# Hybrid encoder step: which gates are projected plainly, a buffer for the LayerNorm's squares, and where the down operands lie

## The chip, the cores and the metric

The kernel runs on one core of one Trainium2 chip. The metric is the device time of one launch in microseconds, median of several executions.

## The reference, cut to what matters

One layer of a hybrid encoder runs on 1024 prompt frames and 64 new frames of another stream, 1088 tokens in all, with model width 1024 in float32. A normalised input `h` is multiplied with one wide matrix. The columns of the product feed four branches of width 512, a SiLU gate for each, and four merge gates of width 1024:

```
h = rms_norm(x, norm_pre);  P = h @ w_in
A: RG-LRU        u_a = lru(conv4(lru_x)) * silu(lru_g)
B: SSD           u_b = rms_norm(ssd(silu(conv4(xbc))) * silu(ssd_z), ssd_norm)
C: conv module   u_c = silu(layer_norm(conv31(glu(cf_in)))) * silu(cf_g)
D: attention     u_d = stick_breaking(q, k, v) * silu(sb_g)
m = sum over b of sigmoid(P_merge_b) * (u_b @ w_down[b])
y = x + rms_norm(m @ w_out, norm_post)
```

The states of the convolutions, of the LRU and of the SSD, and all keys and values, are outputs too.

## The kernel before

Channels lie on the partitions and tokens on the free axis. `hh` and `hl`, each [128, 8, 1088], hold `h` as a rounded high part and the rest (the kernel calls such a pair hi and lo); a product of two such pairs is three matmuls (`mm3`, or the triple at line 721). A column group of 128 is called a chunk; weights come from DRAM by `weights` or `Pair.prepare` and are split into hi and lo by ScalarE and VectorE (`split`, lines 228 and 229).

The stages, in order of time:

1. Head, attention, convolutions: plain projection in three token pieces (`SPL`: 384, 384, 320 tokens). It ends with four chunks by `spill`, which applies SiLU and stores the gate in DRAM. Before the change these are the SSD gates `sz` (C_SZ).
2. Pairs: 20 `Pair` objects, each two chunks by Strassen's scheme of seven products (`ORDER` = 1, 2, 6, 5, 7, 3, 4). The tokens are split in two halves of 544 (`tlo`, `thi`), the contraction in `k0` and `k1`; a product reads one quadrant pair: products 1, 2, 3, 4 read `hh` and `hl` at (k0, tlo), (k1, tlo), (k1, thi), (k0, thi), the others separate tiles T6, T5, T7. A product is 24 matmuls of 272 columns. Two pairs make the LayerNorm gates `cg` (C_CG), two the LRU gates `lg`, 16 the merge gates `mgs`; `done` applies SiLU where asked and stores `r`. Six banks of PSUM serve them.
3. Beside the pairs runs a generator, `chains()`. After each product `step` calls `next(side)`, so that its work is emitted between products: `wait(15)`, then `layer_norm` (four quarters of 272 tokens), `lru` (eight half chunks), `ssd` (nine chunks of 128 tokens: seg, join of the chunk before, scores, norm of the chunk before, turn, off, diag). A `yield` ends a step. There are 140 products, so 140 calls; what is left is called at once after the pairs (line 1078).
4. Down products: for each branch in the order 3, 0, 2, 1 the operand `u` is loaded from DRAM (`uh_d`, `ul_d`), eight output chunks `d` of it are multiplied in the pieces of `SPL`, and VectorE multiplies each with the sigmoid of a merge gate (`load_gate`, tiles `sga`) and adds up in `m`. `us[0]` is loaded into a pool on the right side of SBUF, where the SSD's pool was; `us[1]` and `us[2]` into the places of `hh` and `hl`.
5. Output product, norm and residual in 9 token tiles.

TensorE's instructions keep the order in which the program emits them (`manual_schedule`); the other engines' and the DMA queue's (all DMAs are issued from SP) are ordered by a planner with priorities (`high_priority`). Every queue is in order. A tile of a pool of one buffer is written again only when its last reader is done.

In `layer_norm` the lines that matter are:

```
sq = ln.tile([128, 4, QT], FT, name="lnq")
S.activation(sq, X, AF.Square)                 # line 775
a = fold(sq)                                   # lines 755, 756
yield from wait(2)
p = pg()[:, :QT]
PE.matmul(p, ones, a, start=True, stop=True)   # line 779
...
gh = ln.tile([128, 4, QT], FR, name="lnh", tag="lnq")
split(gh, gw, X)
dma(uh_d[2][:, :, t], gh.bitcast(FT))          # line 793
```

`lnh` and `lnq` are one buffer by their tag. Line 772 is the first matmul of a quarter (the sum for the mean), 773 subtracts the mean, 781 to 789 finish the norm.

Of the kernel before, what the change touches and what calls it, by code (L numbers as in the profile page):

```python
# [8 lines left out]
FT = mybir.dt.float32  # L9
FR = mybir.dt.float32r  # L10
# [35 lines left out]
def encoder_step(ctx, tc, x, prm, win, wdt, wdn, wout, lwa, lwx, ckT, cv_, ssd0, npre, npost, dtb, alog, dskip,  # L46
# [534 lines left out]
    def spill(chunk, dst):  # L581
        def evac(t0, n, p):
            g = tmp.tile([128, NM], FT, name="t3", bufs=3)
            S.activation(g[:, :n], p[:, :n], AF.Silu)  # L584
            dma(dst[:, t0:t0 + n], g[:, :n])
        yield from proj(chunk, evac)

    feed.add(*(spill(C_SZ + c, sz_d[:, c]) for c in range(4)))
    feed.step(1)
    tlo, thi = slice(0, HT), slice(HT, T)  # L590
    k0, k1 = slice(0, 4), slice(4, 8)
# [146 lines left out]
            dma(dst[:, c + e, f * HT:f * HT + HT], r)  # L738
        return Pair(base + c, base + c + 1, done, func or AF.Copy)

    pairs = [stored(C_CG, c, cg_d, AF.Silu) for c in (0, 2)] + [stored(C_LG, c, lg_d, AF.Silu) for c in (0, 2)]
    pairs += [stored(C_MG, 2 * i, mg_d) for i in range(16)]

    def wait(n):
# [4 lines left out]
    def layer_norm():  # L749
        lnp = ExitStack()  # L750
        ln = lnp.enter_context(tc.tile_pool(name="ln", bufs=1, side="right", reuse_waits="tile"))

        def fold(t_):
            a = ln.tile([128, 2, QT], FT, name="lns", bufs=2)
            V.tensor_tensor(a, t_[:, 0:2], t_[:, 2:4], op=OP.add)
            V.tensor_tensor(a[:, 0], a[:, 0], a[:, 1], op=OP.add)
            return a[:, 0]

        def load(q):
            X = ln.tile([128, 4, QT], FT, name="lnx", bufs=2)  # L760
            dma(X, cv_d[:, :, q * QT:q * QT + QT])
            return X, fold(X)

        nxt = load(0)
        yield from wait(3)
        for q in range(4):
            t = slice(q * QT, q * QT + QT)
            X, a = nxt
            gl = ln.tile([128, 4, QT], FT, name="lng")
            dma(gl, cg_d[:, :, t])  # L770
            p = pg()[:, :QT]
            PE.matmul(p, ones, a, start=True, stop=True)
            V.scalar_tensor_tensor(X, p[:, None, :].to_broadcast([128, 4, QT]), -1.0 / 512, X, op0=OP.mult, op1=OP.add)
            sq = ln.tile([128, 4, QT], FT, name="lnq")
            S.activation(sq, X, AF.Square)
            a = fold(sq)
            yield from wait(2)
            p = pg()[:, :QT]
            PE.matmul(p, ones, a, start=True, stop=True)
            rs = ln.tile([128, QT], FT, name="lnr")  # L780
            S.activation(rs, p, AF.Sqrt, bias=eps_t, scale=1.0 / 512)
            V.reciprocal(rs, rs)
            V.tensor_tensor(X, X, rs[:, None, :].to_broadcast([128, 4, QT]), op=OP.mult)
            if q < 3:
                nxt = load(q + 1)
            for c in range(4):
                V.tensor_scalar(X[:, c], X[:, c], P("lg", c), P("lb", c), op0=OP.mult, op1=OP.add)
            S.activation(X, X, AF.Silu)
            V.tensor_tensor(X, X, gl, op=OP.mult)
            gh = ln.tile([128, 4, QT], FR, name="lnh", tag="lnq")  # L790
            gw = ln.tile([128, 4, QT], FR, name="lnl", tag="lng")
            split(gh, gw, X)
            dma(uh_d[2][:, :, t], gh.bitcast(FT))
            dma(ul_d[2][:, :, t], gw.bitcast(FT))
            yield from wait(3)
        lnp.close()


    def lru():
# [31 lines left out]
            pass  # L831
        todo = [(c, j) for c in range(4) for j in range(2)]
        nxt = load(0, 0)
        yield from wait(2)
        for m, (c, j) in enumerate(todo):
            t = slice(j * HT, j * HT + HT)
            xc, xh, xl = nxt
# [201 lines left out]
        p3.close()  # L1039

    def chains():
        yield from wait(15)
        yield from layer_norm()
        yield from lru()
        yield from ssd()
# [22 lines left out]
    for n, pair in enumerate(pairs):  # L1068
# [6 lines left out]
                pairs[n + 1].prepare()  # L1075
            next(side, None)
        pair.run(next_weights, step)
    while next(side, left) is not left:
        pass


    order = (3, 0, 2, 1)
    put = ExitStack()
    ut = put.enter_context(tc.tile_pool(name="ut", bufs=1, side="right", reuse_waits="tile"))

    def load_u(bi, pool, **kw):
        u = pool.tile([128, 2, 4, T], FR, name=f"u{bi}", **kw)
        for e, src in enumerate((uh_d, ul_d)):
            for t0, n in SPL:
                dma(u[:, e, :, t0:t0 + n].bitcast(FT), src[order[bi]][:, :, t0:t0 + n])  # L1090
        return u

    us = [load_u(0, ut, tag="u")]
    nwd = weights(wdn[order[0], 0])
    a1.close()
    ps2.close()
# [2 lines left out]
    def pj():  # L1099
        return ps.tile([128, 512], FT, name="pj3", bufs=6)  # L1100

    tp_ = ctx.enter_context(tc.tile_pool(name="tp", bufs=3, reuse_waits="tile"))
    mp = ctx.enter_context(tc.tile_pool(name="mp", bufs=1, reuse_waits="tile"))
    mt = [mp.tile([128, T], FT, name=f"m{d}") for d in range(8)]
    sgp = ctx.enter_context(tc.tile_pool(name="sgp", bufs=1, reuse_waits="tile"))
# [7 lines left out]
    def down(wh, wl, e, u, t0, n):  # L1113
        p = pj()
        for k in range(4):
            mm3(p[:, :n], wh[:, 4 * e + k, :], wl[:, 4 * e + k, :], u[:, 0, k, t0:t0 + n], u[:, 1, k, t0:t0 + n], k == 0, k == 3)
        return p

    gates = [load_gate(order[0], d) for d in range(8)]
    us += [load_u(1, hp, tag="hh"), load_u(2, hp, tag="hl")]  # L1120
    ml = []
    for bi, b in enumerate(order):
        u = us[bi]
        if bi == 1:
            us.append(load_u(3, ut, tag="u"))
        if bi == 3:
            mh = hp.tile([128, 8, T], FR, name="mh", tag="hh")
            wo0 = hp.tile([128, 8, 1024], FR, name="wo0", tag="hl")
            wo = [[wo0[:, d] for d in range(8)], []]
        for d in range(8):  # L1130
            if d % 2 == 0:
                wh, wl = nwd
            g = gates[d]
            for i, (t0, n) in enumerate(SPL):
                p = down(wh, wl, d % 2, u, t0, n)
                m, gi = mt[d][:, t0:t0 + n], g[:, t0:t0 + n]
                if bi == 0:
                    V.tensor_tensor(m, p[:, :n], gi, op=OP.mult)
                else:
                    V.tensor_tensor(gi, p[:, :n], gi, op=OP.mult)  # L1140
                    if bi < 3:
                        V.tensor_tensor(m, m, gi, op=OP.add)
                    else:
                        V.tensor_tensor(gi, m, gi, op=OP.add)
                        S.activation(mh[:, d, t0:t0 + n], gi, AF.Copy)
                if i == 0 and d % 2 and (d < 7 or bi < 3):
                    nwd = weights(wdn[b, d // 2 + 1] if d < 7 else wdn[order[bi + 1], 0])
            if bi < 3:
                gates[d] = load_gate(order[bi + 1], d)
                continue  # L1150
            l_ = mp.tile([128, T], FR, name=f"ml{d}", tag=f"m{d}")
            V.tensor_sub(l_, g, mh[:, d].bitcast(FT))
            ml.append(l_)
            wo[1].append(sgp.tile([128, 1024], FR, name=f"wp{d}", tag=f"sga{d}"))
            raw = wp.tile([128, 1024], FT, name="w_raw", bufs=2)
            dma(raw, wout[d])
            for e in range(2):
                w = wo[e][d]
                split(w[:, 0:512], w[:, 512:1024], raw[:, e * 512:e * 512 + 512])
    put.close()  # L1160
    ut = ctx.enter_context(tc.tile_pool(name="op", bufs=1, side="right", reuse_waits="tile"))
    gp_bc = ut.tile([128, D], FT, name="gp_bc")
    dma(gp_bc, ap(npost, 0, [[0, 128], [1, D]]))
    for i in range(9):
        r = 128 if i < 8 else 64
        xr = ut.tile([128, D], FT, name="xr", bufs=2)
        dma(xr[:r], x[i * 128:i * 128 + r, :])
        st = tp_.tile([128, 4], FT, name="ost", bufs=2)
        sq = ut.tile([128, 512], FT, name="osq")
        yo = ut.tile([128, D], FT, name="yo", bufs=2)  # L1170
        for e in range(2):
            p = pj()
            for k in range(8):
                w = wo[e][k]
                mm3(p[:r], mh[:, k, i * 128:i * 128 + r], ml[k][:, i * 128:i * 128 + r], w[:, 0:512], w[:, 512:1024],
                    k == 0, k == 7)
            S.activation(sq[:r], p[:r], AF.Square, accum_out=st[:r, e:e + 1])
            es = slice(e * 512, e * 512 + 512)
            V.tensor_tensor(yo[:r, es], p[:r], gp_bc[:r, es], op=OP.mult)
        V.tensor_tensor(st[:r, 0:1], st[:r, 0:1], st[:r, 1:2], op=OP.add)  # L1180
        rstd(st, r, D)
        for e in range(2):
            es = slice(e * 512, e * 512 + 512)
            V.scalar_tensor_tensor(yo[:r, es], yo[:r, es], st[:r, 1:2], xr[:r, es], op0=OP.mult, op1=OP.add)
            dma(y_o[i * 128:i * 128 + r, es], yo[:r, es])
# [63 lines left out]
```

## Time and profile before

| | us |
|---|---|
| median of 3 runs | 1520.71 (1520.14 to 1522.0) |
| profiled execution | 1520.43 |
| its span, first to last instruction | 1518.6 |
| TensorE busy | 1417.0 (93%) |
| VectorE busy | 1060.6 (70%) |
| ScalarE busy | 676.1 (45%) |
| mean granted TensorE clock | 0.972 |

Busy time of TensorE is the union of overlapping matmul records; whether it runs at its pace is read from the count of matmuls in a window. The granted clock is a share of 2.4 GHz, and its two levels are 1.00 and 0.50.

### The profile page before, as it was taken

The page shows a single profiled execution, that of the slowest core. Times are in us where ns is not written, and L with a number is a line of the kernel's source. Part 1 is how long each engine was busy: PE and PEld are TensorE (multiplying, and loading weights), DVE is VectorE, ACT ScalarE, POOL GpSimd, SP SyncE. Part 2 cuts the span into 40 slices and gives each one's busy share as a digit, 9 for nine tenths or more (in the row PEclk, how much of TensorE's full clock was granted, in tenths as well). Part 3 has the DMA queues.
Part 4 walks back from the last instruction along what each step waited for, and adds up shares of the span by engine and source line. Part 5 has one row for each costly group of instructions (what it writes and reads, how often), then busy time and mean ns, then how long its engine had stood idle before and what let it go on. Part 6 is the DMA issues. An engine that isn't in the chain of part 4 may idle for free.

```text
span 1518.6 us, 24934 instructions
## 1 busy us (share of the span) xinstructions
PE 1417.0 (93%) x9665; PEld 1352.7 (89%) x9665; DVE 1060.6 (70%) x1604; ACT 676.1 (45%) x1227; POOL 262.4 (17%) x245
## 2 busy tenths in 40 slices
PE   6999999999999999899788999999999289999998
PEld 6899999999999897899788989999999189999885
DVE  6299799789779977645776867787776324669433
ACT  6324543544454454344556885344444412224211
POOL 0002221231231226322211313131220000000000
PEclk9999999999999999999898999999999589999999
DMA  5222222213213233133444445434343987443322
GB/s 205 74 85 64 69 70 80 82 36 105 84 53 94 65 100 93 51 105 121 161 162 156 149 158 154 141 120 142 118 131 111 329 276 244 148 133 124 111 84 70
DMA packets 121206, 184.41 MB, mean 121 GB/s; under 512 B 22272, under 2 KB 82560, under 8 KB 121088
## 3 DMA queue, kind: packets, MB, share of 16 engines
q1 hardware_dynamic: 121088, 182.82, 37.5%
q8 instruction: 76, 1.25, 0.4%
q14 instruction: 42, 0.34, 0.1%
HBM read 118.00 MB, written 60.59 MB: 118 GB/s over the span
## 4 chain that ended last, share of the span: by engine, by line
PE 43%; DVE 6%; DMA 4%; ACT 4%; issue 1%; SPq 0%; DVEq 0%; ACTq 0%
PE bank L721 19%; PE pj L110 7%; PE pj L111 7%; PE pj L109 7%; DVE w_lo L229 1%; DMA sga<-mgs 1%; ACT w_hi L228 1%; DMA u<-ul 1%; DMA uh<-uoh 1%; DMA ul<-uol 1%; DVE gx L860 1%; ACT L852 1%; PE pg L965 0%; DMA uh<-lnh 0%; PE pg L912 0%
## 5 line engine op out<-in xcount | busy, mean ns | idle before, releaser
L109 PE MATMUL pj<-hh,w_hi 128*128 128x384 f32 (+3 forms) x960 | 317.8, 331 | 6.7 <-ACT t L584 5.4
L110 PE MATMUL pj<-hl,w_hi 128*128 128x384 f32 (+3 forms) x960 | 315.3, 328 | 1.6 <-DVE hl L225 1.6
L111 PE MATMUL pj<-hh,w_lo 128*128 128x384 f32 (+3 forms) x960 | 315.1, 328 | 0.0
L721 PE MATMUL bank<-hh,w_hi 128*128 128x272 f32 x640 | 191.8, 300 | 3.2 <-ACT t L584 1.8
L109 PEld LDWEIGHTS pj<-hh,w_hi 128*128 128x128 f32 x960 | 182.2, 190 | 9.5 <-ACT t L584 5.5
L721 PE MATMUL bank<-hl,w_hi 128*128 128x272 f32 x640 | 186.8, 292 | 0.0
L721 PE MATMUL bank<-hh,w_lo 128*128 128x272 f32 x640 | 186.8, 292 | 0.0
L110 PEld LDWEIGHTS pj<-hl,w_hi 128*128 128x128 f32 x960 | 182.1, 190 | 3.6 <-DVE hl L225 2.5
L111 PEld LDWEIGHTS pj<-hh,w_lo 128*128 128x128 f32 x960 | 181.9, 189 | 0.2
L243 DVE SCALAR_TENSOR_TENSOR cvo<-cbuf,p_t,cvo 128x1118 f32<-128x1118 f32 x120 | 165.5, 1379 | 1.8
L721 PE MATMUL bank<-Th,w_hi 128*128 128x272 f32 x480 | 141.3, 294 | 1.5 <-ACT r L725 1.5
L109 PE MATMUL pj<-u,w_hi 128*128 128x384 f32 (+1 forms) x384 | 126.3, 329 | 13.8 <-DMA u<-uh 13.8
L721 PE MATMUL bank<-Th,w_lo 128*128 128x272 f32 x480 | 138.4, 288 | 0.0
L721 PE MATMUL bank<-Tl,w_hi 128*128 128x272 f32 x480 | 138.2, 288 | 0.0
L110 PE MATMUL pj<-u,w_hi 128*128 128x384 f32 (+1 forms) x384 | 126.4, 329 | 6.4 <-DMA u<-ul 6.4
L721 PEld LDWEIGHTS bank<-hh,w_hi 128*128 128x128 f32 x640 | 123.3, 193 | 5.5 <-ACT t L584 2.0
L111 PE MATMUL pj<-u,w_lo 128*128 128x384 f32 (+1 forms) x384 | 126.3, 329 | 0.0
L721 PEld LDWEIGHTS bank<-hl,w_hi 128*128 128x128 f32 x640 | 123.1, 192 | 0.8
L721 PEld LDWEIGHTS bank<-hh,w_lo 128*128 128x128 f32 x640 | 122.8, 192 | 0.0
L460 POOL TENSOR_SCALAR_AFFINE_SELECT fb<-fb 128x128 f32<-128x128 f32 (+1 forms) x72 | 38.5, 535 | 453.7 <-ACT fb L455 329.3
L101 ACT ACTIVATE w_hi<-w_raw 128x1024 fp32r<-128x1024 f32 x56 | 59.4, 1061 | 113.6 <-PE pj L110 106.5
L463 DVE TENSOR_TENSOR_SCAN fb<-fb,ones 128x128 f32<-128x128 f32 (+8 forms) x68 | 90.1, 1325 | 27.9 <-POOL fb L460 27.8
(339 smaller groups left out, 2982.2 us busy)
## 6 DMA issues: line engine op xcount, KB each, us to landing
w_raw<-in_win_dram SPq DMA_DIRECT2D x80, 512.0 KB, 3.8
mgs<-r SPq DMA_DIRECT2D x64, 272.0 KB, 2.5
sga<-mgs SPq DMA_DIRECT2D x32, 544.0 KB, 3.8
w_raw<-in_wdn_dram SPq DMA_DIRECT2D x16, 512.0 KB, 4.4
u<-uh SPq DMA_DIRECT2D x8, 768.0 KB, 6.6
u<-ul SPq DMA_DIRECT2D x8, 768.0 KB, 10.7
xt<-in_x_dram SPq DMA_DIRECT2D x8, 512.0 KB, 9.2
xbc<-xc SPq DMA_DIRECT2D x8, 512.0 KB, 2.7
```

The lines of the kernel that those rows point to most:

```text
L101: S.activation(hi, r3, AF.Copy)
L109: PE.matmul(out, ah, bh, start=first, stop=False)
L110: PE.matmul(out, ah, bl, start=False, stop=False)
L111: PE.matmul(out, al, bh, start=False, stop=last)
L228: S.activation(hi, src, AF.Copy)
L229: V.tensor_sub(lo, src, hi.bitcast(FT))
L243: V.scalar_tensor_tensor(out[:, :n], b[:, i:i + n], w[:, i:i + 1], out[:, :n], op0=OP.mult, op1=OP.add)
L460: G.affine_select(t_[s, 1024 - w:1024], t_[s, 1024 - w:1024], pattern=[[-1, w]], compare_op=OP.is_gt, fill=fill, base=0, channel_multiplier=1)
L463: V.tensor_tensor_scan(F[:, rev], F[:, rev], ones[:, 0:1].to_broadcast([128, n]), 1.0, OP.mult, OP.mult)
L721: PE.matmul(p, a_[:, k], b_[:, k, s], start=new and k == 0 and z == 0, stop=k == 3 and z == 2, skip_group_check=True)
L852: S.activation(ga, gr, AF.Exp, scale=lm8[:, c:c + 1])
L860: V.tensor_tensor_scan(gx[:, :n], ga[:, :n], gx[:, :n], hp_ if j else 0.0, OP.mult, OP.add)
```

## The change

- The LayerNorm gates are projected plainly in stage 1, and the SSD gates as two pairs, after the two of the LRU gates.
- `chains()` starts without `wait(15)`; in `layer_norm` and `lru` one `wait(2)` each becomes `wait(3)`.
- `lnh` has a buffer of its own.
- The call that finishes the side work after the pairs is moved: one call per piece in the first branch of the down products, the rest at the start of the second.
- `us[0]` and `us[1]` are laid into the four quarters of `hh` and `hl` over (k0, k1) and one token half each; these two operands are multiplied in four pieces of 272 tokens. `us[2]` goes into a tile on the right, loaded at the start of the second branch; `us[3]` into `hl`, loaded at the start of the third. The high part of the mix stays in `hh`, and the output stage's buffers are parts of a tile in the place of `hl`.

```
-    feed.add(*(spill(C_SZ + c, sz_d[:, c]) for c in range(4)))
+    feed.add(*(spill(C_CG + c, cg_d[:, c]) for c in range(4)))
...
-    pairs = [stored(C_CG, c, cg_d, AF.Silu) for c in (0, 2)] + [stored(C_LG, c, lg_d, AF.Silu) for c in (0, 2)]
+    pairs = [stored(C_LG, c, lg_d, AF.Silu) for c in (0, 2)] + [stored(C_SZ, c, sz_d, AF.Silu) for c in (0, 2)]
     pairs += [stored(C_MG, 2 * i, mg_d) for i in range(16)]
...  layer_norm
             a = fold(sq)
-            yield from wait(2)
+            yield from wait(3)
...
-            gh = ln.tile([128, 4, QT], FR, name="lnh", tag="lnq")
+            gh = ln.tile([128, 4, QT], FR, name="lnh")
...  lru
         nxt = load(0, 0)
-        yield from wait(2)
+        yield from wait(3)
...
     def chains():
-        yield from wait(15)
         yield from layer_norm()
...
-    while next(side, left) is not left:
-        pass
...
-    us = [load_u(0, ut, tag="u")]
+    HALVES = tuple((q * QT, QT) for q in range(4))
+
+    class Operand:
+        def __init__(self, b, regions):
+            self.pieces = HALVES if len(regions) == 4 else SPL
+            self.parts = regions
+            for e, src in enumerate((uh_d[b], ul_d[b])):
+                for j in range(len(regions) // 2):
+                    t = slice(j * HT, j * HT + HT) if len(regions) == 4 else slice(0, T)
+                    dma(regions[2 * j + e].bitcast(FT), src[:, :, t])
+
+        def at(self, e, k, t0, n):
+            if len(self.parts) == 2:
+                return self.parts[e][:, k, t0:t0 + n]
+            j = t0 // HT
+            return self.parts[2 * j + e][:, k, t0 - j * HT:t0 - j * HT + n]
+
+    us = [Operand(order[0], [t_[:, k, tlo] for t_ in (hh, hl) for k in (k0, k1)])]
     nwd = weights(wdn[order[0], 0])
...
+    us.append(Operand(order[1], [t_[:, k, thi] for t_ in (hh, hl) for k in (k0, k1)]))
...
-    us += [load_u(1, hp, tag="hh"), load_u(2, hp, tag="hl")]
...
         if bi == 1:
-            us.append(load_u(3, ut, tag="u"))
+            while next(side, left) is not left:
+                pass
+            ut = ctx.enter_context(tc.tile_pool(name="ut", bufs=1, side="right", reuse_waits="tile"))
+            u2 = ut.tile([128, 2, 4, T], FR, name="u2", tag="u")
+            us.append(Operand(order[2], [u2[:, 0], u2[:, 1]]))
+        if bi == 2:
+            us.append(Operand(order[3], [hl[:, k0], hl[:, k1]]))
         if bi == 3:
-            mh = hp.tile([128, 8, T], FR, name="mh", tag="hh")
-            wo0 = hp.tile([128, 8, 1024], FR, name="wo0", tag="hl")
+            wo0 = ut.tile([128, 8, 1024], FR, name="wo0", tag="u")
...
-            for i, (t0, n) in enumerate(SPL):
+            for i, (t0, n) in enumerate(u.pieces):
                 p = down(wh, wl, d % 2, u, t0, n)
                 m, gi = mt[d][:, t0:t0 + n], g[:, t0:t0 + n]
                 if bi == 0:
                     V.tensor_tensor(m, p[:, :n], gi, op=OP.mult)
+                    next(side, None)
...
-    ut = ctx.enter_context(tc.tile_pool(name="op", bufs=1, side="right", reuse_waits="tile"))
-    gp_bc = ut.tile([128, D], FT, name="gp_bc")
+    hf = hp.tile([128, 8, T], FT, name="op", tag="hl")
+    gp_bc = hf[:, 0, :D]
...
-        xr = ut.tile([128, D], FT, name="xr", bufs=2)
+        xr, yo, sq = hf[:, 1 + i % 2, :D], hf[:, 3 + i % 2, :D], hf[:, 5, 0:512]
```

## Rows read from the trace of the kernel before

**Rows 1.** The page's 40 slices of 38 us: busy tenths of TensorE, and its clock

```profile
PE   6999999999999999899788999999999289999998
...
PEclk9999999999999999999898999999999589999999
```

**Rows 2.** Windows: length, then busy us (instructions) of each engine; clock, DMA share, GB/s

```profile
core 0: us, PE busy (x) PEld busy (x) DVE busy (x) ACT busy (x) POOL busy (x), PEclk, DMA share, GB/s
650.40:707.80 57.40, 57.39 (x457) 57.39 (x458) 21.68 (x38) 22.34 (x47) 14.71 (x11) 1.00 0.37 124
707.80:806.40 98.60, 77.42 (x553) 75.00 (x552) 73.55 (x115) 53.16 (x82) 21.78 (x15) 0.88 0.48 160
806.40:932.00 125.60, 120.93 (x931) 119.01 (x929) 89.58 (x140) 99.32 (x174) 31.91 (x22) 0.98 0.44 145
...
1174.40:1219.40 45.00, 9.87 (x57) 6.30 (x56) 14.62 (x35) 19.96 (x24) 0.00 (x0) 0.56 0.96 319
1219.40:1224.00 4.60, 4.60 (x15) 4.60 (x16) 0.56 (x1) 0.00 (x0) 0.00 (x0) 0.51 1.07 365
1224.00:1408.00 184.00, 184.00 (x1117) 184.00 (x1116) 115.20 (x195) 58.99 (x72) 0.00 (x0) 1.00 0.53 175
660.00:680.00 20.00, 20.00 (x161) 20.00 (x161) 7.54 (x12) 7.90 (x17) 5.34 (x4) 1.00 0.28 96
720.00:740.00 20.00, 13.94 (x95) 13.40 (x94) 15.23 (x22) 11.89 (x17) 5.77 (x4) 0.81 0.59 192
...
1240.00:1260.00 20.00, 20.00 (x123) 20.00 (x122) 7.68 (x12) 5.47 (x5) 0.00 (x0) 1.00 0.49 153
```

**Rows 3.** TensorE's waits, 650 to 1225: for whom; us in total, times, longest

```profile
PE pg L779 <- DVE lns L756: 14.9, 3, 6.7
PE pj L109 <- DMA u<-uh: 13.8, 1, 13.8
...
PE pj L110 <- DMA u<-ul: 6.4, 1, 6.4
PE pg L1000 <- DVE yt L995: 6.3, 2, 3.6
PE pg L109 <- ACT bdah L228: 6.3, 1, 6.3
```

**Rows 4.** The chain that ended last, 727 to 738: start, us, what

```profile
727.81 1.21 DVE lnx L789
...
729.05 1.13 ACT lnh L228
...
730.19 3.82 DMA uh<-lnh
...
734.09 1.12 ACT lnq L775
...
735.24 0.73 DVE lns L755
...
735.99 0.45 DVE lns L756
...
736.49 1.28 PE pg L779 x2
```

**Rows 5.** TensorE in order of time, first instruction behind the last pair

```profile
1174.38 0.68 PE L912 MATMUL pg<-lt,tri_gt 64*64 64x256 f32 x4
```

**Rows 6.** The DMA queue (SP) in order of time, 1176 to 1208: start, us of issuing

```profile
1176.16 0.56 SPq L1090 DMA_DIRECT2D u<-uh  x1
1179.79 0.52 SPq L945 DMA_DIRECT2D zc<-sz  x1
...
1203.67 0.58 SPq L1010 DMA_DIRECT2D ul<-uol  x1
...
1207.05 1.91 SPq L1090 DMA_DIRECT2D u<-uh  x3
```

**Rows 7.** DMA issues, 1150 to 1230: count, size, median us to landing

```profile
sga<-mgs SPq DMA_DIRECT2D x9, 544.0 KB, 6.6
```

**Rows 8.** VectorE in order of time, first sums of the LayerNorm

```profile
658.57 0.43 DVE L756 TENSOR_TENSOR lns<-lns 128x272 f32<-128x272 f32 x1
```

More of the change, by code (lines that the diff above doesn't have):

```diff
@@ L1077, in encoder_step @@
         pair.run(next_weights, step)
-    while next(side, left) is not left:
-        pass
     order = (3, 0, 2, 1)
[L1083 to L1091, printed above, removed]
-    us = [load_u(0, ut, tag="u")]
+    HALVES = tuple((q * QT, QT) for q in range(4))
[13 more added lines that the diff above has]
+    us = [Operand(order[0], [t_[:, k, tlo] for t_ in (hh, hl) for k in (k0, k1)])]
     nwd = weights(wdn[order[0], 0])
@@ L1100, in pj, with pg @@
         return ps.tile([128, 512], FT, name="pj3", bufs=6)
-    tp_ = ctx.enter_context(tc.tile_pool(name="tp", bufs=3, reuse_waits="tile"))
+    def pg():
+        return ps.tile([128, 512], FT, name="pg3", bufs=2)
+    us.append(Operand(order[1], [t_[:, k, thi] for t_ in (hh, hl) for k in (k0, k1)]))
     mp = ctx.enter_context(tc.tile_pool(name="mp", bufs=1, reuse_waits="tile"))
@@ L1115, in down @@
         for k in range(4):
-            mm3(p[:, :n], wh[:, 4 * e + k, :], wl[:, 4 * e + k, :], u[:, 0, k, t0:t0 + n], u[:, 1, k, t0:t0 + n], k == 0, k == 3)
+            mm3(p[:, :n], wh[:, 4 * e + k, :], wl[:, 4 * e + k, :], u.at(0, k, t0, n), u.at(1, k, t0, n), k == 0, k == 3)
         return p
     gates = [load_gate(order[0], d) for d in range(8)]
-    us += [load_u(1, hp, tag="hh"), load_u(2, hp, tag="hl")]
-    ml = []
+    mh, ml, wo1 = hh, [], []
     for bi, b in enumerate(order):
@@ L1124, in encoder_step @@
         if bi == 1:
-            us.append(load_u(3, ut, tag="u"))
+            while next(side, left) is not left:
[5 more added lines that the diff above has]
+            us.append(Operand(order[3], [hl[:, k0], hl[:, k1]]))
         if bi == 3:
-            mh = hp.tile([128, 8, T], FR, name="mh", tag="hh")
-            wo0 = hp.tile([128, 8, 1024], FR, name="wo0", tag="hl")
-            wo = [[wo0[:, d] for d in range(8)], []]
+            wo0 = ut.tile([128, 8, 1024], FR, name="wo0", tag="u")
         for d in range(8):
@@ L1153, in encoder_step @@
             ml.append(l_)
-            wo[1].append(sgp.tile([128, 1024], FR, name=f"wp{d}", tag=f"sga{d}"))
+            wo1.append(sgp.tile([128, 1024], FR, name=f"wp{d}", tag=f"sga{d}"))
             raw = wp.tile([128, 1024], FT, name="w_raw", bufs=2)
             dma(raw, wout[d])
-            for e in range(2):
-                w = wo[e][d]
+            for w, e in ((wo0[:, d], 0), (wo1[d], 1)):
                 split(w[:, 0:512], w[:, 512:1024], raw[:, e * 512:e * 512 + 512])
-    put.close()
-    ut = ctx.enter_context(tc.tile_pool(name="op", bufs=1, side="right", reuse_waits="tile"))
-    gp_bc = ut.tile([128, D], FT, name="gp_bc")
+    wo = [[wo0[:, d] for d in range(8)], wo1]
+    hf = hp.tile([128, 8, T], FT, name="op", tag="hl")
+    gp_bc = hf[:, 0, :D]
     dma(gp_bc, ap(npost, 0, [[0, 128], [1, D]]))
@@ L1165, in encoder_step @@
         r = 128 if i < 8 else 64
-        xr = ut.tile([128, D], FT, name="xr", bufs=2)
+        xr, yo, sq = hf[:, 1 + i % 2, :D], hf[:, 3 + i % 2, :D], hf[:, 5, 0:512]
         dma(xr[:r], x[i * 128:i * 128 + r, :])
-        st = tp_.tile([128, 4], FT, name="ost", bufs=2)
-        sq = ut.tile([128, 512], FT, name="osq")
-        yo = ut.tile([128, D], FT, name="yo", bufs=2)
+        st = dq.tile([128, 4], FT, name="ost", bufs=2)
         for e in range(2):
```

## The prediction, made before the change was run

> **What bounds the kernel now.** I read the slices first: TensorE is full nearly throughout, so the question is where it is not. There is a dent from slice 19 to 23 and one deep hole at slices 30 and 31, with a fallen clock in and behind it [rows 1]. Then I cut the time after the attention into stages by windows, at the borders that the order of time gives [rows 2]. An undisturbed window of pairs has 161 matmuls in 20 us, 124.2 ns each, so a product of 24 takes 2.98 us. By that measure: 650 to 708 (19 products) loses next to nothing; 707.8 to 806.4 holds 553 matmuls, worth 68.7 us, in 98.6 us, so 29.9 us are lost; 806 to 932 loses 10.0 us; and from 1174.4 to 1219.4 there are 45.0 us with 57 small matmuls. Behind it 15 matmuls of the down products take 4.6 us at a clock of 0.51; at the later pace (123 in 20 us, 162.6 ns each) they are worth 2.4, so 2.2 us more. From 1224 on TensorE is full. The waits name the causes [rows 3]: 14.9 us in three waits for the LayerNorm's sum of squares, 6.3 us for the first LRU matrix, and in the hole two waits for `u` (20.2 us) besides those of the SSD.
>
> The chain shows why the sum of squares is late [rows 4]: the store of `lnh` takes 3.82 us, and only then does ScalarE square the next quarter (line 775), because `lnq` is the same buffer. Two folds later TensorE goes on. The hole has its order written in the program: 15 + 23 + 34 + 77 yields are 149, so after 140 calls ten calls are left, and the trace agrees: the first instruction behind the last pair is the seg of the chunk of 64 tokens [rows 5]. Those ten calls run alone, each step waiting for the one before, and `us[0]` lies where the SSD's pool was, so its loads start at 1207.05, behind the last store of `uol` at 1203.67 [rows 6].
>
> **The change part by part.**
>
> *Own buffer for the squares, and three steps instead of two.* The store leaves the chain: the square then follows line 773 at once, and TensorE asks a product (2.98 us) later. Of the chain from the norm's end to line 779, what stays is 1.12 + 0.73 + 0.45 us [rows 4] against 9 us of products. So the 14.9 us go. The lower clock goes with them: the stage's mean was 0.88, so about 24% of it ran at the lower level; this is where the 8.7 us lie that remain of the 29.9 beside the two waits. The LRU's wait for its first matrix (6.3 us) gets one more product, so I leave 3.3 us of it.
>
> What is late next is VectorE. It was busy 73.55 us in the stage. Undisturbed pairs need 7.54 us of it in 20 us, or 1.12 per product; 22 products make 24.7, which leaves 48.9 us for the LayerNorm. In the new order this work meets 27 products (24 in four quarters of six, 3 in the handover to the LRU): 48.9 + 30.2 = 79.1 us in a TensorE time of 27 times 2.98 plus 3.1 (25 small matmuls), 83.6 us. That is 95% of an in-order queue. Bounds: at full use nothing is lost; at the share that it had before (75%) the stage would last 105.5 us, 22 us too long. I take 88%, nearer to full because the chain's longest wait is gone: 90 us, 7 us lost. Gain of this stage: 29.9 - 3.3 - 7 = 19.6 us.
>
> *No wait of 15 steps.* The LayerNorm starts beside the first pairs. Its first sum is ready at 658.57 + 0.43 us [rows 8], and its first matmul now stands behind product 4, at about 662: no wait. The plain `cg` spill has the size that the `sz` spill had; both kinds of pairs apply SiLU; the LRU gates come a pair of pairs earlier and the SSD gates are done at product 28 of the 62 that pass before the SSD: all this at nothing.
>
> *The ten calls.* Now 27 + 35 + 77 yields are 139, and the 140th call runs to the end. So nothing is left for the first down branch: the calls there are idle, whatever they are named for; the fill comes from the wait taken out. The hole goes: 45.0 + 2.2 us. The TensorE work in it moves between the last products: 9.87 us busy less the one `u` matmul, at a clock of 0.56, so about 4.7 us at the full one.
>
> *`us[0]` in the quarters of `hh` and `hl`.* Four DMAs of 1.11 MB. Their quarters are last read by products 1 and 2 of the last pair, five products (15 us) and some 3 us of SSD matmuls before the end. At the 365 GB/s that the trace reaches one takes 3.05 us; the first piece needs three, 9.2 us, so about 6 us of reserve if SP issues them in time. SP is in order, and I see it stand from 1176.7 to 1179.79 before a `zc` load [rows 6]; such stops can eat the reserve. Bounds: 0, and the whole load behind the last product (9.2 us, 3 until the last lands, 2.2 of lower clock: 14). I take 2, nearer to 0, since SSD steps now run at the products' pace.
>
> *Gates and `us[1]`.* The `sga` tiles lie on T7 and the pair's buffers; the first are free two products before the end, and 6.6 us from issue to landing [rows 7] plus a sigmoid are covered by six banks of PSUM, 9 us of pieces. `us[1]` (4.46 MB, 12 us) is due a branch later: 46 us (184 us for four). Cost nothing; if all queued ahead of the gates, 3 to 6 us, inside the bounds above.
>
> *`us[2]`, `us[3]`.* `us[3]` adds a wait: its DMA stands on SP until the second branch's last product, with gate and weight loads queued behind it, for which the third branch waits. The load is 12 us of a 46 us branch, so 34 us cover it. `us[2]` is loaded a branch ahead too. In exchange the transfer of a third operand leaves the crowded moment (319 GB/s in the hole). The output stage's tile in `hl` is free with the fourth branch's last product, as `u`'s place was before: nothing.
>
> *Four pieces.* In two branches 16 times 12 groups of three matmuls (3 times 162.6 = 488 ns) become four (4 times 124.2 = 497 ns): 192 times 9 ns, 1.7 us lost. The Trainium skill (TensorE: Matmul & The Clock Gate, "Wait — 56ns, not 53.3ns?") puts a fixed 2.5 ns on each matmul at the full clock; by it the 192 more would cost an estimated 0.5 us and the sum would end 1.2 us lower. The trace's 124.2 ns for 272 columns are 10.9 above 272 / 2.4, so here the row is dearer, and I go by the row.
>
> **The sum.** 19.6 + 45.0 + 2.2 - 4.7 - 2 - 1.7 = 58.4 us. From a span of 1518.6 that leaves 1460.2; 1.8 us lie around the span, so 1462.0 for an execution like the profiled one (1520.43), and the median of the runs stands 0.3 above it: 1462.
>
> **Rivals.**
>
> *R1, the operand load takes the hole's place.* For it: SP stood in just this stretch, and DMA share was 0.96. Against it: 15 to 18 us of lead for 9.2 us. 14 instead of 2 us: 1474.
>
> *R2, VectorE becomes the bound of the LayerNorm.* For it: 95% need. Against it: TensorE's long waits in that stage were for the two named tiles, not for weights or banks [rows 3]. 22 instead of 7 us: 1477. With R1: 1489.
>
> *R3, slower.* Between product 4 and 31 TensorE is stopped often and briefly, and its clock stays at the lower level. At that level a matmul takes 307 against 162.6 ns, so a product costs 2.65 us more; all 27 products so would cost 71 us, less the 7 that VectorE then no longer costs: 1526. It decides from 22 products on. Against it: with waits of up to 6.7 us the window with the lowest clock had 0.81, which is 38% at the lower level [rows 2, 3]. The Trainium skill (TensorE: Matmul & The Clock Gate, "A second HAM failure mode: psum-queue depth-cycling") describes such short idling between groups of matmuls as a cause of an oscillating clock; by that rule this rival gets its chance, and the pairs at 650 to 708, with the same bank cycling and a clock of 1.00, speak against it.
>
> **Chances.** Forecast 0.60, with its own range of 1453 (VectorE at full use, no DMA wait) to 1471 (12 us lost to VectorE, 6 to DMA). R1 0.13, R2 0.14, both 0.04, R3 0.03, nothing moves by 0.2% 0.02 (0.2% is about what a measurement of this kernel can tell from no change), better than 1453 0.04. The range is 1450 to 1484: it takes in the forecast, R1 and R2. Faster 0.95, same 0.02, slower 0.03.
>
> **What would show it.** Line 779 (or its successor) no longer waits 14.9 us, and the square no longer waits for a DMA. The last pair ends near 1160 instead of 1174.4, and the down products begin within 5 us, at a full clock. VectorE stands near 88% beside the first 30 products. Down matmuls of 272 columns come 124 ns apart. The prediction is wrong if a wait for a transfer stands at the first down product, if w_lo or bank waits fill the LayerNorm's stage, or if the clock falls there.

## The result, and the profile after

The changed kernel takes 1486.22 us (median of 4 runs, 1485.71 to 1488.06) against 1521.36 us before on the same chip: a ratio of 0.9767, 95% interval 0.9747 to 0.9787. The profiled execution took 1485.71 us, its span 1483.3 us. The forecast was 1462, range 1450 to 1484: the direction and most of the mechanism came, but 35.3 us of span were gained instead of 58.4.

The page of the changed kernel, its 40 slices (37 us each now): in place of the deep hole of [rows 1] stands a shallow one, and the clock dips in two slices only.

```profile
PE   6999999999999999899979989999999889999997
...
PEclk9999999999999999999989999999999989999999
```

Windows of the changed kernel, columns as in [rows 2]: the LayerNorm beside pairs, the handover to the LRU, the last products with the last SSD steps, the first six down pieces, the stop behind them, and what follows.

```profile
662.50:745.70 83.20, 82.20 (x636) 80.77 (x636) 72.19 (x98) 54.69 (x90) 21.95 (x14) 1.00 0.50 169
745.70:760.00 14.30, 6.02 (x38) 5.49 (x37) 8.99 (x27) 6.68 (x12) 4.65 (x5) 0.73 0.60 202
1131.00:1171.00 40.00, 39.05 (x317) 36.98 (x315) 22.73 (x47) 15.99 (x31) 1.61 (x1) 1.00 0.60 200
1171.00:1180.00 9.00, 8.07 (x64) 8.07 (x65) 2.99 (x7) 2.58 (x5) 0.00 (x0) 1.00 1.00 330
1180.00:1200.00 20.00, 10.91 (x67) 10.68 (x66) 3.95 (x10) 9.25 (x9) 0.00 (x0) 0.74 0.99 374
1200.00:1290.00 90.00, 90.00 (x699) 90.00 (x698) 51.06 (x102) 24.84 (x23) 0.00 (x0) 1.00 0.63 221
```

The first row answers to the 0.88 window of [rows 2]: TensorE is full at a clock of 1.00, with VectorE at 72.19 / 83.2 = 87%. The second and the fifth are the two places here that lose most.

TensorE's waits in the changed kernel, 640 us to the end, columns as in [rows 3]:

```profile
PE pj L109 <- DVE m L1150: 9.1, 1, 9.1
PE pg L109 <- ACT xg L228: 8.1, 1, 8.1
PE pg L912 <- DVE lt L902: 4.5, 1, 4.5
...
PE pj L109 <- ACT rs__12675 L1002: 1.4, 1, 1.4
...
PE pg L779 <- DVE lns L756: 0.3, 1, 0.3
```

The 14.9 us at line 779 have become 0.3, and nothing waits for an operand any more. In their place the down products wait 9.1 us for VectorE's `m`. The chain that ended last shows what that is:

```profile
1178.27 10.44 DMA sga<-mgs
...
1188.73 1.12 ACT sga L1119
...
1189.87 0.45 DVE m L1150
...
1190.37 0.60 PE pj L109
1190.97 0.23 PE pj L110
```

The first merge gate is issued at 1178.27, eight microseconds after the last pair product (its last matmul starts at 1170.1), and takes 10.44 us to land. Six pieces fill the six banks meanwhile, then TensorE stands; behind the stop its matmuls come 0.23 us apart, the lower level of the clock, until 1195.7. The DMA queue in order of time says why the issue is so late:

```profile
1168.29 0.72 SPq L1091 DMA_DIRECT2D hh<-ul  x1
...
1172.14 0.52 SPq L1091 DMA_DIRECT2D hh<-uh  x1
1174.50 0.56 SPq L1009 DMA_DIRECT2D uh<-uoh  x1
1175.47 0.73 SPq L1010 DMA_DIRECT2D ul<-uol  x1
1176.26 0.89 SPq L1091 DMA_DIRECT2D hl<-uh  x1
1177.19 1.03 SPq L1091 DMA_DIRECT2D hl<-ul  x1
1178.27 18.75 SPq L1118 DMA_DIRECT2D sga<-mgs  x10
```

All four transfers of `us[1]` (1088 KB each, line 1091), due a branch later, and the stores of the last SSD norm stand ahead of the gates; SP stood at the store until the norm was computed. The gate stood in a line of transfers: the last quarter of `us[1]`, issued at 1177.19, took 10.2 us, and the gate landed 1.3 us behind it. The row of ten gate loads is not 18.75 us of issuing: in it SP waited 1.6 and 2.7 us for the last two quarters of `us[1]` to land and 8.6 us for VectorE to be done with gates of the first branch.

**Where the missing 23 us are.** Split at the last pair product's end. The forecast put it at 1174.4 - 19.6 + 4.7 = 1159.5 and gave 1460.2 - 1159.5 = 300.7 us to what follows. The trace has 1170.3 and 313.0: 10.8 us are missing before it and 12.3 behind it.

### The profile page after: what moved, and what is told of

Its sections match the earlier page's. It is cut to its first block, busy times and chain, and to the rows that moved or that the text cites. A ratio compares the mean times of both kernels' runs of the same rounds, so it can differ in the third digit from the quotient of the medians.

```text
span 1483.3 us, 25336 instructions
## 1 busy us (share of the span) xinstructions
PE 1413.3 (95%) x9857; PEld 1352.0 (91%) x9857; DVE 1067.1 (72%) x1628; ACT 673.0 (45%) x1225; POOL 263.0 (18%) x245
## 4 chain that ended last, share of the span: by engine, by line
PE 40%; DVE 7%; ACT 4%; DMA 4%; issue 2%; SPq 0%; DVEq 0%; ACTq 0%
PE bank L721 16%; PE pj L109 7%; PE pj L110 7%; PE pj L111 7%; DVE w_lo L229 2%; DMA uh<-uoh 1%; DMA uh<-uah 1%; ACT w_hi L228 1%; DMA sga<-mgs 1%; PE pg L912 1%; DVE r L728 1%; PE pg L965 1%; ACT L852 1%; DVE lnx L787 0%; DVE yz L1005 0%
## 5 line engine op out<-in xcount | busy, mean ns | idle before, releaser
L110 PE MATMUL pj<-hl,w_hi 128*128 128x384 f32 (+4 forms) x1184 | 384.8, 325 | 1.6 <-DVE hl L225 1.6
L109 PE MATMUL pj<-hh,w_hi 128*128 128x384 f32 (+4 forms) x1088 | 354.7, 326 | 8.2 <-ACT t L584 5.5
L111 PE MATMUL pj<-hh,w_lo 128*128 128x384 f32 (+4 forms) x1088 | 352.3, 324 | 0.0
L110 PEld LDWEIGHTS pj<-hl,w_hi 128*128 128x128 f32 x1184 | 225.5, 190 | 3.5 <-DVE hl L225 2.5
L109 PEld LDWEIGHTS pj<-hh,w_hi 128*128 128x128 f32 x1088 | 206.5, 190 | 11.0 <-ACT t L584 5.6
L111 PEld LDWEIGHTS pj<-hh,w_lo 128*128 128x128 f32 x1088 | 206.2, 190 | 0.2
L725 ACT ACTIVATE r<-bank 128x272 f32<-128x272 f32 x160 | 62.0, 391 | 91.1 <-PE bank L721 90.8
L102 DVE TENSOR_TENSOR w_lo<-w_raw,w_hi 128x1024 fp32r<-128x1024 f32 x56 | 70.9, 1266 | 44.4 <-ACT w_hi L101 43.9
L721 PEld LDWEIGHTS bank<-Th,w_hi 128*128 128x128 f32 x480 | 92.1, 192 | 2.6 <-issue 1.2
```

The costliest lines, as they stand in the source:

```text
L102: V.tensor_sub(lo, r3, hi.bitcast(FT))
L109: PE.matmul(out, ah, bh, start=first, stop=False)
L110: PE.matmul(out, ah, bl, start=False, stop=False)
L111: PE.matmul(out, al, bh, start=False, stop=last)
L721: PE.matmul(p, a_[:, k], b_[:, k, s], start=new and k == 0 and z == 0, stop=k == 3 and z == 2, skip_group_check=True)
L725: S.activation(R[to][:, s], p, self.last if j == 4 else AF.Copy)
```

## The experiments

All times are medians, ratios are to the kernel before on the same chip (there it took 1519.85 to 1521.85 us). Where two runs of different chips are compared, the difference by these ratios is given too. "Last pair" is the start of the last matmul of line 721, "rest" is the span less that time, both of the profiled execution.

| kernel | us | ratio (95%) | last pair | rest |
|---|---|---|---|---|
| before | 1521.36 | 1 | 1174.2 | 344.4 |
| after | 1486.22 | 0.9767 (0.9747 to 0.9787) | 1170.1 | 313.2 |
| side work alone | 1501.41 | 0.9877 (0.9862 to 0.9892) | 1172.2 | 328.8 |
| down part alone | 1506.26 | 0.9903 (0.9886 to 0.9920) | 1176.0 | 328.1 |
| before + own buffer | 1511.43 | 0.9934 (0.9919 to 0.9949) | 1164.1 | 342.9 |
| after, buffer shared | 1490.83 | 0.9805 (0.9790 to 0.9819) | 1177.3 | 311.0 |
| after, gates ahead of `us[1]` | 1485.95 | 0.9767 (0.9751 to 0.9784) | 1171.5 | 312.1 |
| after, `us[1]` six chunks later | 1480.80 | 0.9748 (0.9733 to 0.9763) | 1171.3 | 307.7 |
| after, LRU handover of six steps | 1475.33 | 0.9715 (0.9699 to 0.9732) | 1160.0 | 312.2 |
| these two together | 1469.38 | 0.9667 (0.9648 to 0.9685) | 1162.7 | 308.1 |
| with three gates ahead | 1472.22 | 0.9667 (0.9651 to 0.9683) | 1164.3 | 307.6 |
| and six steps before the SSD | 1470.21 | 0.9664 (0.9648 to 0.9681) | 1152.2 | 317.4 |
| after, four pieces everywhere | 1485.37 | 0.9757 (0.9742 to 0.9771) | 1170.2 | 314.6 |

**1. The late gates: put them ahead of `us[1]`.** The theory is the order on SP, the rival the bytes of this stretch.

```
-    us.append(Operand(order[1], ...))
...
-    gates = [load_gate(order[0], d) for d in range(8)]
+    with tc.high_priority(offset=300):
+        gates = [load_gate(order[0], d) for d in range(8)]
+    us.append(Operand(order[1], ...))
```

> The changed kernel with the eight gate loads of the first branch moved ahead of the second operand's loads in the program and given priority over the stores of the last SSD chunk. If the stop of 9.1 us behind the sixth piece of the down products comes from the place of the gate loads on the DMA queue: the stop falls below 2 us, the clock stays near 1.00 there, and the time falls by 9 to 12 us, to 1474 to 1477. If it comes from the bytes that have to pass in any order (about 14 MB around the border): the stop moves to the second operand or to later gates, and the time changes by less than 4 us.

No difference: 1485.95. TensorE's waits of this kernel, and a step of its chain:

```profile
PE pj L109 <- ACT w_hi L101: 5.7, 1, 5.7
```

```profile
1194.24 9.69 DMA w_raw<-in_wdn_dram
```

The stop behind the sixth piece shrank from 9.1 to 1.2 us, but a weight load, issued behind `us[1]` and the next branch's gates, now took 9.69 us to land, and TensorE waited 5.7 us for it. The order alone moves the stop; the rival holds for this run.

**2. Take the bytes out of the stretch.** The gates as in 1, and `us[1]` is laid only at the seventh chunk of the first branch (behind six chunks, not five as the expectation has it):

```
         for d in range(8):
+            if bi == 0 and d == 6:
+                us.append(Operand(order[1], ...))
```

> As x1_gates_first (gate loads ahead and with priority), and the second operand laid into its quarters late, in the program behind the fifth output chunk of the first branch, so that on the DMA queue gates and weights stand ahead of three of its four loads. If in x1 the stop only moved because weights then stood behind the second operand: both stops stay below 3 us, the clock stays near 1.00, 1474 to 1478. If the border is bound by bytes whatever the order: a stop of 5 us or more at some other transfer, 1482 to 1487.

1480.80, between the two expectations: 5.4 us less than after, 2.9 by the ratios, whose intervals overlap. What shows the gain is the trace: the rest is 5.5 us shorter (307.7 against 313.2). TensorE's wait that remains of the stop:

```profile
PE pj L109 <- DVE m L1152: 4.5, 1, 4.5
```

Half the stop of 9.1 us is gone. SP still took one of the four transfers of `us[1]` ahead of the gates, as soon as its quarter was free, and the last norm's stores too; the first gate was issued at 1178.19 and landed 7.16 us later.

**3. The handover from the LayerNorm to the LRU.** In `lru` the wait behind the first load is six steps instead of three:

```
         nxt = load(0, 0)
-        yield from wait(3)
+        yield from wait(6)
```

> The changed kernel with six idle steps instead of three ahead of the LRU's loop; three SSD calls (a join, an idle one, a norm) are then left for the first down branch. If the 8.1 us at the LRU's first matmul is only too little lead for the LRU's loads: the wait is gone, with some 2 us of lower clock, and three calls behind the last pair cost at most 3 us: 1476 to 1481. If the LayerNorm's end moves later by as much (VectorE bound): the wait stays above 4 us, 1484 to 1488.

1475.33, 10.9 us less than after (7.9 by the ratios), a little better than either expectation. The window of the handover in this kernel, beside the second row of the windows above:

```profile
745.70:760.00 14.30, 14.30 (x116) 14.30 (x115) 12.36 (x35) 8.04 (x16) 4.75 (x6) 1.00 0.77 249
```

The wait of 8.1 us is gone and the clock stays at 1.00 (after: 0.73, and 38 matmuls instead of 116). Behind the first LRU matrices the products go on at 758.93 (after: 759.45), but with three more of them done, worth 3 times 2.98 us. Line 912's wait falls too, from 4.5 to 2.5 us in two waits, while the waits for `gr` (line 846) grow from 2.7 to 5.4. Two SSD steps, for which no pair product is left, run among the first down pieces; the rest is 1.0 us shorter all the same. The stop of 9.1 us behind the sixth piece is 5.8 here, though nothing in the down part was changed.

**4. Both together.**

> x9_late_operand and x5_handover together. If the causes add up: 1464 to 1470. If the three left calls collide with the gates on VectorE's queue: 1472 to 1478.

1469.38: 16.8 us less than after, against 5.4 + 10.9 = 16.3 for the two (by the ratios 15.2 against 10.8). Within the noise they add up. The same program was run once more beside the next two runs:

> The combination of the late second operand and the longer handover to the LRU once more, one look, as the measure for the run beside it on the same chip: 1469 to 1471.

It took 1466.1 in its one execution there, so differences of 3 us between runs of different times are not read here.

**5. What is left of the stop.** Three gates ahead of the first branch, the others each three chunks before their use.

```
-        gates = [load_gate(order[0], d) for d in range(8)]
+        gates = [load_gate(order[0], d) for d in range(3)]
...
+            if bi == 0 and d + 3 < 8:
+                gates.append(load_gate(order[0], d + 3))
```

> That combination with three gates ahead of the first branch and the others each three chunks before their use. Theory: what is left of the stop (3.2 us and some 2 of lower clock) is there because eight gate loads of 544 KB are in flight at once and land together; the first took 9.71 us. With three in flight it lands in 4 to 6 us and the stop goes: 1464 to 1467. Rival: the bytes that have to pass in this stretch are the limit, and a later gate is late instead: 1468 to 1471.

1472.22, no gain. The wait and the first gate's transfer in its chain:

```profile
PE pj L109 <- DVE m L1154: 2.6, 1, 2.6
```

```profile
1167.98 9.07 DMA sga<-mgs
```

The gate took 9.07 us to land with four loads issued together instead of eight (9.71 and 8.56 us in the two executions of 4). The theory that eight loads in flight make the first one late falls. Two quarters of `us[1]` were issued ahead of the gates in both programs, the second of them right ahead. The transfers issued from 1167 to 1168.5 in this run (count, size, us to landing), and ScalarE's first sigmoids of a gate:

```profile
hh<-uh SPq DMA_DIRECT2D x1, 1088.0 KB, 8.4
sga<-mgs SPq DMA_DIRECT2D x1, 544.0 KB, 9.1
```

```profile
1177.08 1.11 ACT L1118 ACTIVATE sga<-sga 128x1088 f32<-128x1088 f32 x1 [1.93 <-DMA sga<-mgs]
1178.43 1.11 ACT L1118 ACTIVATE sga<-sga 128x1088 f32<-128x1088 f32 x1 [0.25 <-DMA sga<-mgs]
```

The quarter, issued at 1167.33, landed at 1175.7, the first gate 1.3 us behind it, and the gates then 1.35 us apart. They do not land together: each lands behind what was issued ahead of it, and the loads behind the first gate do not hold it up. So what is left of the stop stands behind the two quarters of `us[1]`; how much goes when these are moved too was not run.

**6. A longer handover to the SSD too.** In addition, the `wait(3)` behind the SSD's first `cur.decay()` becomes `wait(6)`.

> The same with the wait of the SSD behind its first decay raised from three steps to six as well, so that three more steps of the SSD fall between down products. Theory: the 2.5 us for the SSD's first matrix go, and the steps that fall among the down products cost no more there than among the pairs: 2 to 3 us less than the run with three gates. Rival: among pieces of 1.5 us the steps stand closer than their chain takes, and each costs a wait of 1 to 3 us: the same or up to 6 us more.

1470.21: the same. The pairs end twelve microseconds earlier than in run 5 (1152.2 against 1164.3), the rest is ten longer (317.4 against 307.6). TensorE in order of time at the border, and VectorE there:

```profile
1152.74 0.38 PE L941 MATMUL pg<-ident,xb 128*64 128x128 f32 x2
1163.10 0.57 PE L109 MATMUL pj<-hh,w_hi 128*128 128x272 f32 x1 [9.97 <-issue]
```

```profile
1161.66 0.68 DVE L937 TENSOR_TENSOR xdt<-pg,dt 64x512 f32<-64x512 f32 x1 [6.31 <-DMA uh<-uoh]
1162.31 0.68 DVE L938 TENSOR_TENSOR xdd<-pg,dtd 64x512 f32<-64x512 f32 x1
```

The profile names no releaser for the 9.97 us. The trace has TensorE's sequencer waiting there until 1163.04 for a quarter of `us[0]`, which had landed at 1138.3, and for a semaphore of VectorE; the two lines of VectorE show of what: the first down product starts 0.11 us after `xdd` ends. `xdt` and `xdd` read a PSUM tile of the pairs' pools, and the down products use new pools over the same banks. `xdt` shares its buffer with `uoh` by a tag, so it waited for the store of the norm before. Neither expectation had this: the steps behind the border cost little, a step that straddles it costs the whole gain. In the changed kernel the same border costs the 1.4 us of `rs__12675`, the last reader of such a bank.

**7. The two halves of the change by themselves.** Side work alone is before with the swapped gates, no `wait(15)`, waits of 3 and the own buffer; the down part is as before. The down part alone is after with those five edits undone.

```
-    feed.add(*(spill(C_SZ + c, sz_d[:, c]) for c in range(4)))
+    feed.add(*(spill(C_CG + c, cg_d[:, c]) for c in range(4)))
...
-        yield from wait(15)
```

> The kernel before with only the side work's part of the change: LayerNorm gates plain, SSD gates as pairs, no 15 idle steps, three steps for two, own buffer; the tail as before. No SSD call but the last norm is left behind the pairs, but the first operand still lies where the SSD's pool was. If the drained calls made most of the hole: it shrinks from 45 to 17 to 22 us (the last norm, its stores, the operand's load), 1488 to 1495. If the place of the operand is what holds the hole open, because its loads wait for the SSD's last store and then for 13 MB of three operands: 25 to 35 us of hole, 1498 to 1508.

> The changed kernel with the LayerNorm's part undone: SSD gates plain, LayerNorm gates as pairs, 15 idle steps at the start, two steps where the change has three, the shared buffer. Ten SSD steps are then really left for the first down branch. If the two parts add up, the LayerNorm's 18 us are lost and the losses at the later handovers (some 7 us) with them: 1494 to 1499. If the ten steps cannot run between the pieces because VectorE's queue stands behind the multiplication with a late gate: a wait at the end of the first branch or a longer stop, 1500 to 1510.

1501.41 and 1506.26: 1.23% and 0.97% gained, together 2.20%, and 2.33% with both. In the first no step of the SSD is left behind the pairs, and yet the old operand place keeps a hole. TensorE's waits there:

```profile
PE pj L109 <- DMA u<-uh: 15.0, 1, 15.0
...
PE pj L110 <- DMA u<-ul: 5.5, 1, 5.5
```

In the second the ten steps run between down pieces, as the change provides. TensorE's waits there:

```profile
PE pg L955 <- DMA Sb<-in_ssd_dram: 16.3, 1, 16.3
PE pg L779 <- DVE lns L756: 15.5, 3, 7.0
```

A step among the down pieces needs a load (`Sb`) that stands on SP behind the gates, and TensorE's fixed order puts the down products behind that step. The two halves add up within the noise, and each alone leaves a stop of 15 us or more where both together leave 9.1: one empties the border, the other feeds it.

**8. The buffer alone, and the change without it.** Before with `lnh` in a buffer of its own, and after with the shared one.

```
-            gh = ln.tile([128, 4, QT], FR, name="lnh", tag="lnq")
+            gh = ln.tile([128, 4, QT], FR, name="lnh")
```

> The kernel before, with only the buffer of its own for the LayerNorm's squares. If the store in the chain was what stopped TensorE: the 14.9 us at line 779 fall below 3, the clock in that stage rises above 0.95, and the time falls by 16 to 20 us, to 1501 to 1505. If the third step per half quarter and the earlier start are needed as well, because VectorE is nearly full: 5 to 10 us.

> The changed kernel with the one buffer for squares and high part as before, all else as changed. If the store is the cause and the third step gives only its 3 us: three waits of 2 to 3 us come back at line 779, with some lower clock, 6 to 12 us slower than the changed kernel, 1492 to 1498. If the longer spacing alone takes the LayerNorm off the path: within 3 us of the changed kernel.

The buffer is worth 10 us in the old order (1511.43) and 4.6 in the new one (1490.83 against 1486.22; 5.8 by the ratios): as the second expectation of the first run has it, and a little less than the 6 to 12 us of the other run's first. The waits for the sum of squares in the two, and in the first that for the LRU's first matrix:

```profile
PE pg L109 <- ACT bdah L228: 8.1, 1, 8.1
PE pg L779 <- DVE lns L756: 4.6, 2, 3.7
```

```profile
PE pg L779 <- DVE lns L756: 6.2, 3, 3.0
```

Either the buffer, or the third step with the new order, takes 9 to 10 of the 14.9 us of [rows 3], and only both reach 0.3: with the store out of the chain, two products in the old order are still too little cover. The third step was not tried apart from the new order.

**9. The price of four pieces.**

```
-            self.pieces = HALVES if len(regions) == 4 else SPL
+            self.pieces = HALVES
```

> The kernel after the change with four pieces of 272 tokens in all four branches instead of two of them. By the trace of the changed kernel a group of four pieces is 4 times 126 = 504 ns against 488 for three, so two more branches (192 groups) cost 3.1 us: 1489 to 1490. By the forecast's rate (4 times 124.2 = 497 ns) it is 1.7 us: 1488. Rival: matmuls are not what sets these branches (weights, gates or VectorE's sums are), then no difference: 1486.

1485.37, no difference from after. The third branch has three pieces in after; VectorE's sums there in order of time, twelve sums or four chunks apart:

```profile
1285.35 0.56 DVE L1155 TENSOR_TENSOR m<-m,sga 128x384 f32<-128x384 f32 x1
...
1309.35 0.56 DVE L1155 TENSOR_TENSOR m<-m,sga 128x384 f32<-128x384 f32 x1
```

The same branch in four pieces in this run, sixteen sums apart:

```profile
1286.13 0.44 DVE L1155 TENSOR_TENSOR m<-m,sga 128x272 f32<-128x272 f32 x1
...
1310.22 0.44 DVE L1155 TENSOR_TENSOR m<-m,sga 128x272 f32<-128x272 f32 x1
```

That is 6.00 against 6.02 us a chunk. Before, three pieces took 5.94:

```profile
1279.79 0.56 DVE L1142 TENSOR_TENSOR m<-m,sga 128x384 f32<-128x384 f32 x1
...
1303.55 0.56 DVE L1142 TENSOR_TENSOR m<-m,sga 128x384 f32<-128x384 f32 x1
```

So the pieces cost 0.3 to 1.3 us in 16 chunks. My 3.1 us were wrong, and so was the 488 ns that they rest on: 162.6 ns was worked out from the count of matmuls in a window [rows 2], and a window counts the records that cross its borders too, 123 where 20 us at this pace hold 121.

## Why the prediction was wrong, and where it was right

**The step that failed: "Gates and `us[1]` ... Cost nothing; if all queued ahead of the gates, 3 to 6 us, inside the bounds above."** Just that queueing came about, and it cost 9.1 us of stop and about 2.4 of lower clock behind it (5.3 us at 227 instead of some 125 ns a matmul), some 11.5 in all. Three readings behind the term failed. I counted from when the gates' tiles come free; what counted was the issue: SP is in order, and the last norm's store was not issued before 1174.50, with half of `us[1]` behind it and still ahead of the gates. I took 6.6 us from issue to landing out of a calmer stretch [rows 7]; it was 10.44, because the gate landed behind all that was issued ahead of it. And six banks covered 9 us as written, but counted from the first down product at 1171.93, against a gate ready at 1189.85. Runs 1 and 2 show the cause as order and bytes together: order alone moves the stop to a weight, and moving the operand away as well halves it. The 2.1 to 3.2 us of this wait that stay in the two executions of run 4 stand behind the two quarters of `us[1]` that SP still takes ahead of the gates (run 5).

**The second: "The LRU's wait for its first matrix (6.3 us) gets one more product, so I leave 3.3 us of it."** It was 8.1 us, and the clock fell with it (0.73 in that window). One more product does not cover this chain. VectorE first splits weights of a coming pair; SP stands before the next weight load until that is done, and behind it issues the LRU's loads one after the other, `xl` behind four others; TensorE waits for `xg`, ScalarE's split of `xl`. VectorE's line is from the chain that ended last, the others from the order of time:

```profile
748.02 2.68 DVE w_lo L229 x2
```

```profile
750.73 0.34 SPq L688 DMA_DIRECT2D w_raw<-in_win_dram  x1
...
753.66 0.58 SPq L825 DMA_DIRECT2D xl<-xls  x1
```

```profile
756.68 0.66 ACT L228 ACTIVATE xg<-xl 128x544 fp32r<-128x544 f32 x1 [1.02 <-DMA xl<-xls]
```

```profile
757.39 0.59 PE L109 MATMUL pg<-xg,bdah 128*128 128x272 f32 x1 [8.11 <-ACT xg L228]
```

The own buffer alone lengthens the wait at this place too, from 6.3 to 8.1 us (run 8); that it does so because fewer stops in the LayerNorm leave less time to the loads is argued, not shown. Run 3 shows what the handover was worth: three more steps give 10.9 us (7.9 by the ratios), and the last pair is at 1160.0, where the forecast had it. SP issues these loads at the same times there; it is the three products that cover them.

The time itself went missing on both sides of this place. Up to it the stage gained less than said. The first pair matmul behind the LRU's first matrices, after 31 products, and before, after 41:

```profile
759.45 0.43 PE L721 MATMUL bank<-Th,w_hi 128*128 128x272 f32 x1
```

```profile
806.28 0.43 PE L721 MATMUL bank<-hh,w_hi 128*128 128x272 f32 x1
```

That is 46.8 less 10 times 2.98, or 17.0 us (19.6 forecast); the handover took more than I left it, VectorE less than the 7 us that I set aside (79.1 / 0.88 less 83.6 is 6.3, so 7 was a little much by my own sum). From there to the end of the pairs 109 products took 411.0 us, before 99 took 368.2: 42.8 less 29.8 are 13.0 us, where I had 4.7 for the ten SSD steps. Line 912's 4.5 us (1.3 before) are part of these 8.3; why it waits longer in the new order is open; with run 3's cover it is 2.5.

**The SSD steps.** Right that nothing is left for the first down branch: the calls there are idle. Run 7 shows that, used, they would have cost: 16.3 us for one load.

**`us[0]`, R1.** It landed in time, and the 2 us were not needed. R1 ("the operand load takes the hole's place") happened with another transfer: it was `us[1]` and the gates. That its 14 us lie near the 11.5 is luck, for no down product waited for its operand. With the side work as changed, the whole down part of the change is worth 15.6 us of the rest (328.8 to 313.2); the move of `us[0]` was not tried by itself.

**VectorE, R2, and the clock, R3.** VectorE stood at 87% beside the LayerNorm's products and TensorE was full, so R2 did not come. The 88% that I said were meant for 27 products with the handover; there, from 662.10 to 759.45, VectorE was busy 81.17 of 97.35 us, 83%, so its work was forecast well (79.1) and the likeness of the shares is in part luck. The clock was 1.00 over the whole LayerNorm, so R3 did not either. The Trainium skill's cause for an oscillating clock (TensorE: Matmul & The Clock Gate, "A second HAM failure mode: psum-queue depth-cycling") did not show here: this stretch cycles its banks as before, and TensorE was busy 82.20 of its 83.20 us.

**Four pieces.** 1.7 us said, 0.3 to 1.3 measured: my row, read at a window's borders, was a little too dear. The Trainium skill's fixed 2.5 ns a matmul (TensorE: Matmul & The Clock Gate, "Wait — 56ns, not 53.3ns?"), an estimated 0.5 us for 192 matmuls, lies inside.

**The rest behind the pairs.** Of the 12.3 us missing there, 11.5 are the gates, 1.4 the bank of the last norm; 2 for `us[0]` and up to 1.4 for pieces were set aside and not used. Some 1 to 3 us are not assigned; down chunks in the third branch at 6.00 instead of 5.94 us are part of it.

## What to carry to other kernels

When a hole at a stage border is closed, list every transfer that the border must pass, in the order in which its one queue will issue them, with the wait of each ahead of the urgent one; "free in time" is not "issued in time", and here a load landed only behind what was issued ahead of it. A prefetch due much later belongs behind the stretch, not just behind the urgent load: reordering alone moved the stop, spreading the bytes removed half of it. When a stall is taken out, look for cover at the next handover: here one number (3 to 6) was worth 8 to 11 us.

## What the runs showed that I had not expected

A PSUM bank handed from one pool to the next can carry a wait that the profile puts down to "issue": 9.97 us, found by looking at which engine ends an instruction just then (run 6). Gate loads of 544 KB landed in the order of their issue, 1.35 us apart, so the first one's 8.6 to 10.4 us are a place in a line and no slowness of its own. A weight load issued behind ten of them in the changed kernel could not leave before 1197.07.
